# Second layer's input blocks without the row factor 1/rms, which multiplies the products' results

## The chip, the core and the metric

The kernel runs on one core of one Trainium2 chip. The core has a matrix engine (TensorE, PE in the profile; PEld are its weight loads), a vector engine (VectorE, DVE), a scalar engine (ScalarE, ACT), GpSimd (POOL) and SyncE (SP), which here issues nearly all DMAs. The engines run their own instruction streams and wait for one another on semaphores. The metric is the device time of one execution in microseconds, median of the runs.

## The reference

A decoder trunk of two layers on x (1024 tokens by 1024 channels, f32). Each layer normalizes the rows, projects, mixes, gates and projects back:

```python
for i in range(DEPTH):
    hn = rms_norm(h, ln_g[i])            # h * rsqrt(mean(h*h, -1) + EPS) * g
    proj = jnp.einsum('bsd,de->bse', hn, w_in)
    u, q_mem, gate = ...
    y = diff_attention(u, ...) if i == 0 else multiscale_pool(u, ...)
    m = memory_attention(q_mem, mem_n, w_kv[i])
    z = jnp.concatenate([y, m], axis=-1) * jax.nn.silu(gate)
    h = h + jnp.einsum('bse,ed->bsd', z, w_out[i])
return rms_norm(h, final_g)
```

Layer 1 is differential attention with 12 heads of 128. Layer 2 pools u over windows of 2, 4, 8 and 16 tokens in four groups of 384 channels and mixes each group with a 384 by 384 matrix. Both have a memory attention of four heads over 256 memory tokens.

What matters here: the factor 1/rms belongs to a token (a row of h), the gain g to a channel. In a projection, sum over d of h[s,d] * r[s] * g[d] * w[d,e], the factor r[s] can be taken out of the sum and multiply the result.

## The kernel before, in words

All activations lie with channels on the 128 partitions and tokens in the free dimension: h is 8 tiles (d = 0 to 7) by two halves of 512 tokens. Half 1 is computed first. Each f32 operand is split in a high part (rounded by an ACT copy) and a low part (a DVE or POOL difference), and a product of f32 accuracy is three matmuls (`mm3`, L126 to L128): high by high, high by low, low by high.

**The order of the work.** `plan` fills a list of jobs. Each has a load (DMA of weights, splits) and a run that yields steps on PE; the load of job i + 1 is called ahead of the run of job i. PE's order is the program's; the other engines' instructions are put in order by a scheduler that goes by priority (program order, with `high_priority(offset=SOON)` to draw some forward) and its own estimate of times, and so are the DMA issues on SP.

**Layer 1's output projection** is `out_jobs(0)` (L1551). For half 1 and then half 0 it goes through three rounds of d (0 to 2, 3 to 5, 6 and 7), each over all 16 tiles of z (`chunk`, L1588). When a d is complete, `finish` (L1623) loads the matching part of x into a tile `res` (L1629, two slots in layer 1), adds it to the bank (L1640), squares the sum and adds it to a running sum of squares (`accumulate_square`, L503), and stores h to DRAM (L1648). `means` (L1654) turns the sum of squares into row means on PE (L251) and takes the inverse root in a chain of small DVE operations (L225 to L242); `spread` (L1657) broadcasts the factor over the partitions with PE (`row_spread`, L524). For half 1 both run within half 0's first round. `blocks_first` (L1273) then scales half 1's eight tiles by gain and factor (L1265) and splits them, between the chunks of half 0's second round.

**Layer 2's input projection** uses Winograd's form of Strassen's algorithm with 7 products for 8. Rows are the two halves of tokens, columns two weight tiles (a pair), and the sum over d is cut at d = 4. The seven products take the blocks 11, 21 (half 1, d below and from 4), t1 = x12 - x11, t2 = x22 - t1, t3 = x22 - x12, t4 = x21 - t2 and 22 of the hidden state, four tiles each. `product` (L1140) makes one: 12 matmuls from a box of split weights (`split_box`, L1126; six boxes, prepared four products ahead; weights come by DMA into three raw buffers, L1130). Results are joined on the way out of the banks: `keep` (L1188) holds p1, u2 and u3, and `evac0` and `evac1` give the four finished halves of the pair to `mem_query_keep`, `gate_keep` or `pooled_keep`. `land` (L1213) is the step that takes a bank out: an ACT copy, or a DVE addition when there is something to add.

**The passage between the two** is `plan_mixing` (L1038). Four pairs of a memory query and a memory gate (`firsts`) and a pair of u tiles (`lead`) run their products 1 and 2 first, as these need only half 1's blocks. `means0(0)` stands behind the first product and `spread0(0)` behind the third. `spread0(0)` calls `blocks_second` (L1280), with an order of DVE's work written out by hand: scale the eight tiles of half 0 (L1294), form t1, t2, t3, t4 (L1297), split them and 22 (L1257 and L1258). Then come products 6, 7, 5, 4, 3 of the four pairs and the lead, and four groups, each with its pairs of u and gate tiles and its mixing products (`group`, L1466).

**The memory units** (`mem_units`, L696) of layer 2 run between these products, at steps counted from the mark "out0" and written out as a list (L1538): scores with a softmax, transposes, values. Their operands come by DMA into the pool "mem1", whose memory is that of the pool "out0" before it.

**The pooling** (`pooled_keep`, L1420) adds u shifted by 1, 2, 4 and 8 (L1446, the first on POOL), subtracts u (L1451) and splits (L1460, L1461).

## Time and profile before

| | |
|---|---|
| median of 3 runs | 1838.45 us (1836.51 to 1844.82) |
| the profiled execution's own time | 1839.47 us |
| its span | 1837.7 us |
| mean granted PE clock | 0.986 |
| DMA | 188.68 MB, mean 103 GB/s |
| output projection of layer 1 ends | about 1207.9 us |
| groups of layer 2 end, output projection of layer 2 begins | about 1636 us |

The span is what the profiler saw of one execution; its time is 1.8 us longer. Busy time is the time in which an engine has an instruction under way; matmuls are pipelined and their ends are modelled, so they overlap a little. A row of a table of stretches gives the stretch, its length, the busy time (and number of instructions) of PE, PEld, DVE, ACT and POOL, the granted PE clock (1.00 is full), the share of the DMA engines and GB/s. A row of waits gives the waiting engine, tile and line, what ended the wait, the total, the number and the longest. A timeline row gives start, duration, engine, line, operation, output and inputs, shape and count; in brackets is the idle time of the engine before it. A row of a line's instructions gives the shortest, median and longest duration in ns. `pmq_pga12` is the pair of memory query 0 and gate tile 12, with a letter for the bank's role: x (products 1 and 2), y (6), z (7, 4), v (5, 3).

### The profile page before, as it was taken

The page shows a single profiled execution, that of the slowest core. Times are in us where ns is not written, and L with a number is a line of the kernel's source. Part 1 is how long each engine was busy: PE and PEld are TensorE (multiplying, and loading weights), DVE is VectorE, ACT ScalarE, POOL GpSimd, SP SyncE. Part 2 cuts the span into 40 slices and gives each one's busy share as a digit, 9 for nine tenths or more (in the row PEclk, how much of TensorE's full clock was granted, in tenths as well). Part 3 has the DMA queues.
Part 4 walks back from the last instruction along what each step waited for, and adds up shares of the span by engine and source line. Part 5 has one row for each costly group of instructions (what it writes and reads, how often), then busy time and mean ns, then how long its engine had stood idle before and what let it go on. Part 6 is the DMA issues. An engine that isn't in the chain of part 4 may idle for free. (4 is left out here: it accounts for less than half of the span.)

```text
span 1837.7 us, 24949 instructions
## 1 busy us (share of the span) xinstructions
PE 1747.2 (95%) x8634; PEld 1453.9 (79%) x8634; DVE 1219.4 (66%) x2421; ACT 942.2 (51%) x1770; POOL 640.7 (35%) x555
## 2 busy tenths in 40 slices
PE   7799999999999999999989999997999999989997
PEld 5688888888888888888788787875788777767875
DVE  7766676667667667665447677778876767754423
ACT  6667566657657656743246556554533332234422
POOL 4334334343334334333151143500133433413452
PEclk9899999999999999999999999998999999999998
DMA  5011111111111111112462787852312121146542
GB/s 175 33 35 47 39 54 58 35 49 56 35 58 47 35 58 58 36 52 75 149 209 80 241 283 251 285 170 84 111 61 89 61 83 67 54 153 223 164 160 92
DMA packets 83982, 188.68 MB, mean 103 GB/s; under 512 B 9456, under 2 KB 17360, under 8 KB 83856
## 3 DMA queue, kind: packets, MB, share of 16 engines
q1 hardware_dynamic: 81600, 183.08, 30.1%
q10 hardware_dynamic: 2160, 3.75, 0.5%
q8 instruction: 68, 1.11, 0.3%
q14 instruction: 58, 0.48, 0.1%
q0 software_dynamic: 96, 0.26, 0.1%
HBM read 155.29 MB, written 31.77 MB: 102 GB/s over the span
## 5 line engine op out<-in xcount | busy, mean ns | idle before, releaser
L863 ACT ACTIVATE e<-e,st 128x640 f32<-128x640 f32 (+4 forms) x192 | 148.3, 773 | 93.6 <-DVE st L854 92.5
L119 POOL TENSOR_TENSOR wl_o<-wf_o,wh_o 128x288 fp32r<-128x288 f32 (+1 forms) x80 | 110.1, 1377 | 219.9 <-ACT wh_o L116 185.4
L874 POOL TENSOR_SCALAR e<-e,st,coef 128x640 f32<-128x640 f32 (+4 forms) x96 | 89.3, 930 | 169.3 <-DVE st L873 164.6
L1583 DVE TENSOR_TENSOR zr<-zf,zr 128x512 fp32r<-128x512 f32 x132 | 112.4, 866 | 35.4 <-ACT zr L1582 33.7
L119 DVE TENSOR_TENSOR wl_o<-wf_o,wh_o 128x480 fp32r<-128x480 f32 (+1 forms) x80 | 60.3, 754 | 110.6 <-ACT wh_o L116 107.7
L903 ACT CAST wth<-wt 128x512 fp32r<-128x512 f32 (+2 forms) x168 | 71.9, 428 | 107.7 <-PE wt L900 81.4
L1582 ACT CAST zr<-zf 128x512 fp32r<-128x512 f32 x132 | 81.6, 620 | 82.0 <-DMA zf<-z 58.0
L116 ACT CAST wh_o<-wf_o 128x768 fp32r<-128x768 f32 (+1 forms) x80 | 70.1, 876 | 99.4 <-PE ob L127 42.4
L904 DVE TENSOR_TENSOR wtl<-wt,wth 128x512 fp32r<-128x512 f32 (+2 forms) x168 | 83.1, 495 | 55.9 <-ACT wth L903 55.5
L854 DVE CUSTOM_DVE_ANT_0 e<-s,mask 128x512 f32<-128x512 f32 (+2 forms) x192 | 109.2, 583 | 14.5 <-PE s L849 12.4
L849 PE MATMUL s<-kb,qa 128*128 128x512 f32 (+2 forms) x288 | 99.2, 351 | 7.8 <-DVE kb L801 7.2
L126 PE MATMUL ga<-hh,wh_ga 128*128 128x512 f32 x256 | 104.0, 406 | 0.0
L127 PE MATMUL ga<-hl,wh_ga 128*128 128x512 f32 x256 | 100.9, 394 | 0.0
L128 PE MATMUL ga<-hh,wl_ga 128*128 128x512 f32 x256 | 100.9, 394 | 0.0
L849 PE MATMUL s<-kb,qlo 128*128 128x512 f32 (+2 forms) x288 | 98.8, 350 | 0.0
L878 DVE SCALAR_TENSOR_TENSOR e<-e,st,e 128x640 f32<-128x640 f32 (+4 forms) x96 | 80.5, 838 | 14.9 <-POOL e L874 14.2
L126 PE MATMUL k<-hh,wh_k 128*128 128x512 f32 x192 | 80.9, 421 | 8.7 <-ACT wh_k L116 8.7
L126 PE MATMUL oa<-zr,wh_o 128*128 128x512 f32 x192 | 75.8, 395 | 6.2 <-ACT zr L1582 4.2
L128 PE MATMUL oa<-zr,wl_o 128*128 128x512 f32 x192 | 75.3, 392 | 4.7 <-DVE wl_o L119 2.6
L126 PE MATMUL v<-hh,wh_v 128*128 128x512 f32 x192 | 79.6, 414 | 0.0
L127 PE MATMUL k<-hl,wh_k 128*128 128x512 f32 x192 | 76.3, 397 | 3.3 <-DVE hl L499 3.3
L126 PE MATMUL q<-hh,wh_q 128*128 128x512 f32 x192 | 79.2, 413 | 0.0
(1225 smaller groups left out, 5517.9 us busy)
## 6 DMA issues: line engine op xcount, KB each, us to landing
zf<-z SPq DMA_DIRECT2D x132, 256.0 KB
wf_o<-in_w_out SPq DMA_DIRECT2D x64, 384.0 KB
wf_ga<-in_w_in SPq DMA_DIRECT2D x16, 512.0 KB
wf_o<-in_w_out SPq DMA_DIRECT2D x16, 512.0 KB
wf_q<-in_w_in SPq DMA_DIRECT2D x12, 512.0 KB
wf_v<-in_w_in SPq DMA_DIRECT2D x12, 512.0 KB
z<-rs SPq DMA_DIRECT2D x24, 256.0 KB
z<-z SPq DMA_DIRECT2D x24, 256.0 KB
```

What stands on the lines that cost most here:

```text
L119: eng.tensor_tensor(wl[:, c], wf[:, c], wh[:, c].bitcast(F32), op=ALU.subtract)
L126: nc.tensor.matmul(out, sh, mh, start=first, stop=False, skip_group_check=more)
L127: nc.tensor.matmul(out, sh, ml, start=False, stop=False, skip_group_check=more)
L128: nc.tensor.matmul(out, sl, mh, start=False, stop=last, skip_group_check=more)
L849: nc.tensor.matmul(sc[m][:, w], q[half][part][:, m, qs], k[kh][:, m, w], start=(part == 0), stop=(part == 1),)
L854: nc.vector.tensor_tensor_reduce(out=es[m][:, lo:hi], in0=sc[m][:, : hi - lo], in1=self.mask[:, S - n + lo : S - n + hi], scale=1.0, scala ...
L863: nc.scalar.activation(es[m][:, :n], es[m][:, :n], AF.Exp, bias=least[m], scale=-1.0, accum_out=st[:, 2, m : m + 1],)
L874: nc.gpsimd.tensor_scalar(es[1][:, :n], es[1][:, :n], st[:, 3, 1:2], self.coef[:, 1:2], op0=ALU.mult, op1=ALU.mult,)
L878: nc.vector.scalar_tensor_tensor(es[0][:, :n], es[0][:, :n], st[:, 3, 0:1], es[1][:, :n], op0=ALU.mult, op1=ALU.add)
L904: nc.vector.tensor_tensor(wl[:, lo:hi], t[:, lo:hi], wh[:, lo:hi].bitcast(F32), op=ALU.subtract)
L1582: nc.scalar.copy(z[:, 0, :], zf)
L1583: nc.vector.tensor_tensor(z[:, 1, :], zf, z[:, 0, :].bitcast(F32), op=ALU.subtract)
```

## The change

1. **Blocks without 1/rms.** In layer 1's `finish`, the residual sum is made in place in the tile `res`, which now has three slots and is stored from there. ACT writes a copy scaled by the second layer's gain, and `blocks(half, d)` at once makes what can be made of it: the splits of 11 and 21 for half 1; t1 for half 0 with d below 4; t2 and t3 with d from 4.
2. **Late blocks last.** `blocks_last` makes t4 and 22. It stands behind products 1 and 2 of the first two pairs.
3. **The factor on the results.** `spread` copies the factor of each half into a kept tile `rs1`. `land` multiplies with it on DVE: from the bank where there is nothing to add, in place behind the addition otherwise. `keep` (p1, u2, u3) stays without it. The gates' tanh and product now read the tile and not the bank.
4. **Leads over two sets of banks.** Products 1 and 2 of two pairs take turns, one on the banks `pj`, one on `sb`. The lead pair of u tiles no longer runs ahead but in the order of the other pairs.
5. **Means behind the leads.** `means0(0)` stands behind all eight leading products, `spread0(0)` behind product 7 of the first pair, and the mark "out0" there too. The memory units' steps from that mark are 8 lower, one of them 10. Against the first pair's product 6 the first unit then stands 8 steps later.
6. The pooling's edge tile has one slot instead of two, and the squares' tile one instead of two in layer 1.

```diff
-        lead = self.pair(u1(0), u1(1))
-        lead["home"] = lambda: (self.epool, "p1", 1)
-        for p in firsts + [lead]:
+        for p in firsts:
             p["early"] = (1, 2)
-        for i, p in enumerate(firsts):
-            self.product(p, 1)
+        for i in (0, 2):
+            for n in (1, 2):
+                for p, bank in zip(firsts[i : i + 2], (self.pj, self.sb)):
+                    self.product(p, n, bank)
             if i == 0:
-                self.between(lambda: means0(0))
-            if i == 1:
-                self.between(lambda: spread0(0))
-            self.product(p, 2)
-        self.mark("out0")
-        self.product(lead, 1, self.sb)
-        self.product(lead, 2)
+                self.between(self.blocks_last)
+        self.between(lambda: means0(0))
         for p in firsts:
             for n in (6, 7, 5, 4, 3):
-                self.product(p, n, self.sb if n == 6 and p is firsts[0] else None)
+                self.product(p, n)
+                if n == 7 and p is firsts[0]:
+                    self.between(lambda: spread0(0))
+                    self.mark("out0")
...
-    def land(self, t, bank, more):
-
+    def land(self, t, half, bank, more):
+
+        by = self.rs1[:, half * HALF : (half + 1) * HALF]
         with self.tc.high_priority(offset=SOON):
-            if more is None:
-                self.nc.scalar.copy(t, bank)
-            else:
+            if more is not None:
                 self.nc.vector.tensor_tensor(t, bank, more, op=ALU.add)
+                bank = t
+            self.nc.vector.tensor_tensor(t, bank, by, op=ALU.mult)
...
-            if more is not None:
-                self.land(g, bank, more)
-            x = bank if more is None else g
-            nc.scalar.activation(th, x, AF.Tanh, scale=0.5)
-            nc.vector.scalar_tensor_tensor(g, th, 1.0, x, op0=ALU.add, op1=ALU.mult)
+            self.land(g, half, bank, more)
+            nc.scalar.activation(th, g, AF.Tanh, scale=0.5)
+            nc.vector.scalar_tensor_tensor(g, th, 1.0, g, op0=ALU.add, op1=ALU.mult)
...
+    def blocks(self, half, d):
...
+        i = d % 4
+        if half:
+            self.split_block(("11", "21")[d // 4], i, h[1, d], 2 * d, 2 * d + 1, nc.vector)
+            return
+        x11, x21 = h[1, i], h[1, 4 + i]
+        x12 = h[0, i]
+        if d < 4:
+            nc.vector.tensor_tensor(x11, x12, x11, op=ALU.subtract)
+            self.split_block("t1", i, x11, 48 + 2 * i, 49 + 2 * i, nc.vector)
+            return
+        x22 = h[0, d]
+        nc.vector.tensor_tensor(x11, x22, x11, op=ALU.subtract)
+        self.split_block("t2", i, x11, 16 + 2 * i, 17 + 2 * i, nc.vector)
+        nc.vector.tensor_tensor(x12, x22, x12, op=ALU.subtract)
+        self.split_block("t3", i, x12, 24 + 2 * i, 25 + 2 * i, nc.vector)
+
+    def blocks_last(self):
...
+        for i in range(4):
+            nc.vector.tensor_tensor(h[1, 4 + i], h[1, 4 + i], h[1, i], op=ALU.subtract)
+            self.split_block("t4", i, h[1, 4 + i], 44 + i, 40 + i, nc.vector)
+        for i in range(4):
+            self.split_block("22", i, h[0, 4 + i], 32 + i, 36 + i, nc.vector)
...
-            r = pool.tile([P, HALF], F32, tag="res", bufs=2 + layer, name=f"res{nm}")
+            r = pool.tile([P, HALF], F32, tag="res", bufs=3, name=f"res{nm}")
             if layer == 0:
                 nc.sync.dma_start(r, a["x"][half, :, d, :])
...
+                h = r
...
             if layer == 0:
                 nc.sync.dma_start(self.h_dram[d][:, cols], h)
+                if half == 0 and d >= 4:
+                    f = pool.tile([P, HALF], F32, tag=f"hk{d}", name=f"hf{nm}")
+                else:
+                    f = self.slot(32 + (d if half else 8 + d), f"hf{nm}", F32)
+                nc.scalar.activation(f, h, AF.Copy, scale=self.ln_g[1][:, d : d + 1])
+                self.hid[half, d] = f
+                self.blocks(half, d)
...
+            cols = slice(half * HALF, (half + 1) * HALF)
+            if layer == 0:
+                self.keep_spread(half, self.rs1[:, cols])
                 return
```

`blocks_first`, `blocks_second`, `scale_hidden` and `h_order` go.

More of the change, by code (lines that the diff above doesn't have):

```diff
@@ L1085, in plan_mixing @@
             t = 3 * gi
+            pairs(u1(t), u1(t + 1))
             if gi == 0:
-                for n in (6, 7, 5, 4, 3):
-                    self.product(lead, n)
                 self.mark("mem1")
-            else:
-                pairs(u1(t), u1(t + 1))
             pairs(gate1(t), u1(t + 2))
@@ L1188, in keep @@
         def keep(name, a, b=None):
-            pool, tag, bufs = p["home"]() if name == "p1" and "home" in p else (self.epool, "ev", 6)
-            t = pool.tile([P, HALF], F32, tag=tag, bufs=bufs, name=f"{name}{nm}")
+            t = self.epool.tile([P, HALF], F32, tag="ev", bufs=6, name=f"{name}{nm}")
             with self.tc.high_priority(offset=SOON):
-                self.land(t, a, b)
+                if b is None:
+                    nc.scalar.copy(t, a)
+                else:
+                    nc.vector.tensor_tensor(t, a, b, op=ALU.add)
             p[name] = t
@@ L1223, in evac @@
             f = self.epool.tile([P, HALF], F32, tag="ev", bufs=6, name=f"mqf1{m}{half}")
-            self.land(f, bank, more)
+            self.land(f, half, bank, more)
             self.nc.sync.dma_start(self.mq_dram[1][m][:, half * HALF : (half + 1) * HALF], f)
@@ L1429, in evac @@
             u = box["u"]
-            self.land(u[:, PAD + half * HALF : PAD + (half + 1) * HALF], bank, more)
+            self.land(u[:, PAD + half * HALF : PAD + (half + 1) * HALF], half, bank, more)
             box[half] = True
@@ L1453, in pooled @@
             )
-            e = pool.tile([P, PAD], F32, tag="edge", bufs=2, name=f"edge{t}")
+            e = pool.tile([P, PAD], F32, tag="edge", name=f"edge{t}")
             b = win - 1
@@ L1532, in other_layers @@
             with self.pool("ev") as self.epool:
+                self.rs1 = self.epool.tile([P, S], F32, name="rs1")
                 with self.pool("out0") as self.opool:
@@ L1628, in finish @@
                 ssum[half] = []
-            r = pool.tile([P, HALF], F32, tag="res", bufs=2 + layer, name=f"res{nm}")
+            r = pool.tile([P, HALF], F32, tag="res", bufs=3, name=f"res{nm}")
             if layer == 0:
                 nc.sync.dma_start(r, a["x"][half, :, d, :])
-                if half == 0 and d >= 4:
-                    h = pool.tile([P, HALF], F32, tag=f"hk{d}", name=f"hn{nm}")
-                else:
-                    h = self.slot(32 + (d if half else 8 + d), f"hn{nm}", F32)
-                self.hid[half, d] = h
+                h = r
             else:
@@ L1642, in finish @@
             self.accumulate_square(
-                pool, h, ssum[half], d, nm, (("ssum", 1), ("ssum_", 1), ("sqt", 2)),
+                pool, h, ssum[half], d, nm, (("ssum", 1), ("ssum_", 1), ("sqt", 1 + layer)),
                 alone=layer == 1 and half == 0,
@@ L1657, in spread @@
         def spread(half):
-            if layer == 0 and half:
-                bc = self.opool.tile([P, HALF], F32, tag="bc", name=f"bc{half}")
-                hs["first"] = self.blocks_first(self.keep_spread(half, bc))
+            cols = slice(half * HALF, (half + 1) * HALF)
+            if layer == 0:
+                self.keep_spread(half, self.rs1[:, cols])
                 return
-            if layer == 0:
-                with self.tc.high_priority(offset=SOON):
-                    self.blocks_second(self.row_spread(half))
-                return
-            cols = slice(half * HALF, (half + 1) * HALF)
             if half:
@@ L1684, in out_jobs @@
                         self.between(lambda f=(means, spread)[kk // 4]: f(1))
-                    if layer == 0 and half == 0 and r == 1:
-                        self.between(lambda: next(hs["first"]))
         return means, spread
```

73 lines of the change are left out of this document (4 added, 69 removed).

## The prediction

> **What bounds the kernel now.** I read the page's busy shares first, then a table of busy times by stretch, the PE's waits in the stretches that the change touches, and the timeline around the longest wait.
>
> ```profile
> span 1837.7 us, 24949 instructions
> PE 1747.2 (95%) x8634; PEld 1453.9 (79%) x8634; DVE 1219.4 (66%) x2421; ACT 942.2 (51%) x1770; POOL 640.7 (35%) x555
> ```
>
> PE is busy 95% of the span, so the change can only win from the missing 5% or lose by making more of it. The stretches say where it lies:
>
> ```profile
> core 0: us, PE busy (x) PEld busy (x) DVE busy (x) ACT busy (x) POOL busy (x), PEclk, DMA share, GB/s
> 1130.00:1160.00 30.00, 27.64 (x125) 22.37 (x124) 28.06 (x46) 18.83 (x31) 14.85 (x8) 1.00 0.62 196
> 1160.00:1207.90 47.90, 47.90 (x213) 39.64 (x213) 33.23 (x42) 25.68 (x40) 17.47 (x13) 1.00 0.84 293
> 1207.90:1272.40 64.50, 48.71 (x209) 37.93 (x207) 53.88 (x98) 31.73 (x61) 0.22 (x2) 0.89 0.33 106
> 1220.00:1256.00 36.00, 28.61 (x119) 21.57 (x117) 35.67 (x59) 20.79 (x37) 0.22 (x2) 0.98 0.23 71
> 1256.00:1268.00 12.00, 4.26 (x14) 3.54 (x15) 8.47 (x15) 2.28 (x4) 0.00 (x0) 0.50 0.51 160
> 1280.00:1320.00 40.00, 39.39 (x199) 31.79 (x198) 36.24 (x71) 20.95 (x54) 5.75 (x4) 1.00 0.34 110
> 1272.40:1384.00 111.60, 107.97 (x534) 88.43 (x534) 94.55 (x167) 50.38 (x120) 26.40 (x19) 1.00 0.25 84
> 1384.00:1429.00 45.00, 45.00 (x199) 37.02 (x198) 24.55 (x37) 13.90 (x23) 12.99 (x11) 1.00 0.27 91
> 1384.00:1636.00 252.00, 242.63 (x1053) 196.53 (x1052) 178.44 (x224) 77.45 (x125) 90.29 (x67) 1.00 0.22 74
> 1429.00:1456.00 27.00, 25.18 (x110) 20.14 (x109) 23.82 (x28) 9.09 (x14) 13.82 (x10) 1.00 0.18 54
> 1501.00:1529.00 28.00, 24.46 (x105) 19.29 (x104) 25.29 (x27) 8.35 (x13) 14.35 (x10) 1.00 0.14 45
> 1576.00:1604.00 28.00, 25.75 (x112) 20.58 (x111) 25.84 (x28) 7.94 (x13) 15.98 (x9) 1.00 0.17 52
> ```
>
> Layer 1's output projection ends at 1207.9. The next 64.5 us, ten leading products and the first pair's last five, have 48.71 us of PE work: 15.8 idle. From 1220 to 1256 DVE works 35.67 of 36 us, so PE waits for DVE there. The memory units and first u tiles (1272.4 to 1384) lose 3.6 us, the groups behind them (1384 to 1636) 9.4, mostly in three short stretches where DVE is 88 to 92% busy.
>
> ```profile
> PE ms L126 <- ACT mq L629: 8.5, 1, 8.5
> PE pmq_pga12z L126 <- DVE u3pmq_pga L1219: 4.2, 1, 4.2
> PE pmq_pga15x L126 <- ACT p1pmq_pga L1217: 0.7, 1, 0.7
> PE ms_h L251 <- DVE ssq L516: 0.7, 1, 0.7
> ```
>
> ```profile
> 1256.13 0.33 SPq L1137 DMA_DIRECT2D wf_pmq_pga14b<-in_w_in  x1
> 1256.55 0.38 SPq L636 DMA_DIRECT2D mkv<-mk  x1
> 1263.46 0.58 PE L126 MATMUL ms<-mkvr,mq 128*128 128x256 f32 x1 [8.48 <-ACT mq L629]
> ```
>
> Two waits hold 12.7 of the 15.8 us. The fourth block sum is split late, as DVE is full; and the memory operands' load leaves SP only at 1256.55, right behind a weight load whose buffer DVE had been slow to free, and reaches PE 6.9 us later. Behind these waits the granted clock is 0.50 (1256 to 1268): 4.26 us of PE work there would need half, another 2.1.
>
> **The change, part by part.** *Second-layer block sums from 1208 on.* Let T be 1207.9 to 1384, 176.1 us, DVE 53.88 + 94.55 = 148.4. Its unit prices:
>
> ```profile
> 1219.01 2.72 DVE L1294 SCALAR_TENSOR_TENSOR hn<-hn,gains,bc_h 128x512 f32<-128x512 f32 x4 [1.78 <-PE bc_h L528]
> 1251.20 1.90 DVE L1258 TENSOR_TENSOR xt4l<-hn,xt4h 128x512 fp32r<-128x512 f32 x3
> L1217 ACT COPY u<-u_u4x x1: 587/587/587, 1421.1 to 1421.1; 128x512 f32<-128x512 f32 x1
> ```
>
> Scalings run at 0.68 us each (2.72/4), two-input operations at 0.61 ((1.90 - 0.69)/2, a single one shows 0.69). The eight scalings go: -5.4. Block sums with d below 6 need no 1/rms any more and are made in the projection: four differences and four splits for t1, the same for t2 and t3 with d = 4 and 5; 16 x 0.61 = -9.8. Six pairs land in T with four evacuations each; every one gets a DVE multiplication, 24 x 0.61 = +14.6 (a multiplication like this isn't in the trace; the split has the same shape and two inputs). DVE's sum hardly moves: 147.8.
>
> What moves is when it falls due. Before, nothing from scaling on could start until PE had the row means, about 1219; now only d = 6, 7 is left at 1207.9 (8 operations, 4.9 us), and t4 and 22 (12, 7.3 us) follow behind the first two pairs' leads. A product is 12 matmuls, 12 x 45.00/199 = 2.7 us: t2 is wanted after eight, at +22, t4 after eleven and the means, at +32. By +22 DVE owes 4.9 and 17 operations more (two residual sums, two sums of squares, six lead splits, four multiplications, three for product 6): 15.3 us. By +32 come 7.3 and six more (products 7, 5, 4; u2, u3): 26.3 and the means' small chain. It keeps up.
>
> PE's floor in T is 176.1 - 15.8 - 3.6 - 2.1 = 154.6. DVE at 147.8 would be 96% of that. The best stretch with this mix, 1280 to 1320, has DVE 90.6% busy and PE losing 0.6 us. At that fill T takes 147.8/0.906 = 163.1: **-13.0**. Ends: the floor, -21.5; or the memory wait left over with its clock and half the rest, 154.6 + 8.5 + 2.1 + 4.3 = 169.5, so -6.6; I take -5 as the bad end, a little beyond that.
>
> *Leads over two sets of banks, means behind them.* The three 0.7 us waits for ACT to copy p1 (one row above stands for them) and the one at the means go; they are in the 15.8. The means' chain of small DVE operations now has two products, 5.4 us, before spread needs it; what waits is the first multiplication with the second half's factor, and behind it on DVE the next pair's splits. The factor's copy costs ACT one instruction like the 0.587 above: hidden, as ACT is 49% busy in 1207.9 to 1272.4. Without that cover PE would wait up to 5 us once.
>
> *The memory units* start eight steps later against the first pair. Scores come after thirteen products, 35.4 us, and about 2 for means and spread: near 1246. Their load, 6.9 us ahead, must leave SP by 1239. It stands in SP's queue behind the weight load that needs the second pair's boxes split, which needs box slots freed by products that end about 1234 to 1237. So it is nearly even: 0 to 4 us of wait, inside the 8.5 that 163.1 leaves above the floor.
>
> *Output projection.* Gone is a burst that cost PE something:
>
> ```profile
> 1140.02 5.94 DVE L1265 SCALAR_TENSOR_TENSOR hn<-hn,gains,bc 128x512 f32<-128x512 f32 x8
> 1148.99 0.50 PE L128 MATMUL oa<-zr,wl_o 128*128 128x512 f32 x1 [1.95 <-DVE wl_o L119]
> L1257 ACT CAST x11h<-hn x4: 612/615/620, 1140.8 to 1143.6; 128x512 fp32r<-128x512 f32 x4
> ```
>
> Scaling (eight) and splitting half 1 in one go left PE 2.4 us idle in 1130 to 1160 (30.00 - 27.64). Now they are spread over the ends of the rounds: 8 splits, 8 operations for t1, 8 for t2 and t3, 24 for the old 16. The densest place is half 0's second round end, where d = 3, 4, 5 come at once: ten operations, 6.1 us, in the stretch 1160 to 1207.9, where DVE has 47.90 - 33.23 = 14.7 us to spare. ACT gains sixteen scaled copies, at 0.615 like the cast above 9.8 us over the projection, beside its 54% there (25.68 of 47.90). On SP nothing is added: the 16 loads of x and 16 stores of h stay; only the store now reads the tile that the load filled, so a slot of res is free one store later. With three slots each is asked for again a whole round later, so this is hidden; if not, a round's last sum is late, and behind it only copies and splits. I put -2.4 for the old burst, +2.4 for the new one: **0** (-2.4 to +4).
>
> *The groups, 1384 to 1636.* Ten pairs land, 40 multiplications, 24.4 us more for DVE, which has 252 - 178.4 = 73.6 to spare. Where it is full, it hurts: each short stretch gets about six (3.7 us), so 23.82, 25.29 and 25.84 become 27.5, 29.0, 29.5 in 27, 28 and 28 us: 3.0 over.
>
> ```profile
> PE pga_u5z L126 <- DVE u2pga_u L1219: 1.8, 1, 1.8
> PE pga_u8z L126 <- DVE u2pga_u L1219: 1.8, 1, 1.8
> PE pga_u8v L126 <- DVE gap L1241: 1.6, 1, 1.6
> PE pga_u11v L126 <- DVE gap L1241: 1.1, 1, 1.1
> L1128 DVE TENSOR_TENSOR box<-s2pga_u,box 128x512 fp32r<-128x512 f32 x6 | 5.9, 980 | 3.4 <-ACT box L1127 3.4
> L1219 DVE TENSOR_TENSOR gap<-pga_u5v,u2pga_u 128x512 f32<-128x512 f32 x1 | 0.7, 691 | 1.4 <-PE pga_u5v L128 1.4
> ```
>
> The waits on u2 get one u multiplication more in front, +0.6 in each of three groups, +1.8. The two waits on the gate may go: its bank was free after tanh and a product, now after one multiplication, -2.7. Thirty of the forty read two SBUF tensors, as the box split does, which takes 0.98 on average here; operations with a bank as one input stay at 0.69. Fifteen fall into the full stretches: 15 x 0.29 = 4.4, a third of it on PE's path, +1.5. Sum 3.0 + 1.8 - 2.7 + 1.5 = 3.6, taken as **+3.5** (-2.7 to +12, half of 24.4).
>
> [...]
>
> **Sum.** -13.0 + 0 + 3.5 = -9.5 against the profiled execution, 1839.47 us (span 1837.7): 1830.0. The median of the runs, 1838.45, is 1.0 lower: 1829.0.
>
> **The rivals.** (a) *The memory wait stays.* SP's queue keeps the load behind the weights. T then gains 6.6, not 13.0: -6.6 + 3.5 = -3.1, 1835.4. For it: the weight load ahead of it still needs the second pair's boxes, as before. Against: what held the weight load was DVE's full stretch, which is lightened.
>
> (b) *Slower: the multiplications reach PE.* Each lies between a result and its reader, u to the pooled sums, gate to its product. Where nine tenths of the 24.4 us reach PE, it is +22.0 - 13.0 = +9.0, 1847.5; it turns slower from 13.0/24.4 = 53%. For it: PE waits for DVE in all three full stretches. Against: from 1384 to 1429 PE loses nothing with DVE at 24.55 of 45, so about half of the multiplications have room.
>
> (c) *Better: T near its floor, groups free.* The stall falls to a third of what 163.1 leaves, 2.8: T -18.7, groups 0: -18.7, 1819.8. For it: 1280 to 1320 lost only 0.6 at 90.6%. Against: four such stretches in a row would be needed, with DVE at 147.8 of 157.4.
>
> (d) [...] If each of the thirty meets POOL at its share, 90.29/252 = 36%, and then waits out a long one, as one split did (2.43 us, 1.74 over 0.69), 30 x 0.36 x 1.74 = 18.8 us of DVE are lost; with half on PE's path instead of the 1.5, groups cost 2.1 + 9.4 = 11.5: -1.5, 1837.0.
>
> ```profile
> 1436.27 2.43 DVE L1128 TENSOR_TENSOR box<-s2pga_u,box 128x512 fp32r<-128x512 f32 x1
> ```
>
> [...]
>
> **How the numbers follow.** Forecast 0.48, (a) 0.15, (b) 0.13, (c) 0.17, (d) 0.07. A measurement of this kernel can tell about 0.5%, 9.2 us, from no change, so faster means below 1829.3. The forecast lies on that bound; as its term of -13.0 has more room below (to -21.5) than its other terms above, I count 0.31 of 0.48 as faster; with (c) 0.48. Slower takes (b) and 0.03 of the rest: 0.16. Same: 0.36. All unknown costs at their good ends give -21.5 - 2.4 - 2.7 = -26.6 (1812), at their bad ends -5 + 4 + 12 = +11 (1849); leaving out (b)'s upper part and the last of (c) takes 1814 to 1843.
>
> **What would show it.** Right: from 1208 on no wait for the fourth block sum, a memory wait under 4 us, clock 1.00 throughout, T near 163 us with DVE about 90% busy, no 0.7 us waits on p1; 1130 to 1160 without the wait on wl_o, at most one new wait at half 0's second round end; in the groups PE's idle time 12 to 14 us instead of 9.4, its waits on u2 longer, on the gate's product gone. Wrong: the wait on the memory operands still 8 us with a clock of 0.50 behind it (a); PE idle in the groups over 25 us (b); under 3 us of waits in T (c); multiplications beside POOL at 1.5 us or more (d).

## The result, and the profile after

The changed kernel takes 1852.57 us (median of 4 runs, 1849.81 to 1852.87), the kernel before 1838.45 (1836.51 to 1844.82): a ratio of 1.0067, 95% interval 1.0041 to 1.0094. It is slower by over half a per cent, where the prediction had 1829.0.

The page of the profiled execution after, whose own time is 1852.87 us (granted clock 0.981, before 0.986):

```profile
span 1851.1 us, 24987 instructions
PE 1760.9 (95%) x8634; PEld 1463.2 (79%) x8634; DVE 1265.1 (68%) x2467; ACT 947.9 (51%) x1779; POOL 643.6 (35%) x557
```

The span is 13.4 us longer. To find them I cut both spans at the same instructions: the first matmul of layer 1's output projection, the first product of the first pair, product 1 of the gate pair 2, that of the gate pair 11, the first matmul of layer 2's output projection, the end. The table of stretches of the kernel before:

```profile
1025.50:1207.90 182.40, 177.98 (x786) 145.32 (x785) 134.40 (x179) 99.98 (x158) 72.52 (x50) 1.00 0.79 263
1207.90:1385.30 177.40, 157.97 (x747) 127.40 (x746) 149.73 (x267) 82.11 (x181) 26.62 (x21) 0.96 0.29 93
1385.30:1604.80 219.50, 211.52 (x919) 171.67 (x918) 154.09 (x193) 68.35 (x111) 84.33 (x62) 1.00 0.22 73
1604.80:1634.30 29.50, 28.11 (x122) 22.40 (x121) 21.37 (x27) 9.10 (x15) 5.16 (x4) 1.00 0.19 57
1634.30:1837.70 203.40, 183.07 (x809) 148.74 (x807) 76.15 (x124) 72.29 (x105) 75.93 (x58) 0.97 0.52 170
```

and of the changed kernel:

```profile
1024.80:1216.80 192.00, 182.18 (x785) 147.43 (x784) 146.11 (x192) 113.87 (x183) 73.07 (x52) 0.98 0.75 249
1216.80:1389.90 173.10, 161.04 (x748) 131.29 (x748) 145.31 (x258) 75.59 (x167) 29.02 (x21) 0.96 0.28 92
1389.90:1615.20 225.30, 213.89 (x920) 172.54 (x919) 188.69 (x230) 65.38 (x107) 81.76 (x62) 0.99 0.21 71
1615.20:1642.50 27.30, 27.30 (x122) 22.48 (x121) 24.41 (x32) 10.54 (x16) 7.02 (x5) 1.00 0.20 58
1642.50:1851.10 208.60, 187.30 (x809) 150.73 (x807) 77.09 (x124) 72.03 (x105) 76.00 (x58) 0.95 0.51 167
```

The first number behind the stretch is its length, the next PE's busy time; length less busy time is PE's idle time, and a lower clock shows as a longer busy time (PE did 10 matmuls in a busy 3.41 us at 0.50, 17 at 1.00). Layer 1's output projection grew by 9.6 us (5.4 of it idle, 9.82 against 4.42; of the 4.2 busy, two drops of the clock to half, at 1125 and 1204, make 3.4). T, the second row, shrank by 4.3: PE's idle time fell by 7.4 (19.4 to 12.1), but its busy time rose by 3.1, since four short drops now lie where PE works, while the one long drop before, 1254.4 to 1268.1, lay for the most part under the wait of 8.5 us. The groups grew by 5.8, their last pair shrank by 2.2, layer 2's output projection, where no code was changed, grew by 5.2; what lies ahead is 0.7 shorter. That is the 13.4.

PE's waits in T after:

```profile
PE mt L679 <- DVE me L670: 4.0, 2, 2.3
PE bc_h L528 <- DVE rsyh L242: 2.6, 1, 2.6
PE mo L694 <- DVE mwl L685: 2.0, 1, 2.0
PE pga_u2v L126 <- DVE pool L1405: 2.0, 1, 2.0
PE ms L126 <- ACT mkvr L643: 0.7, 1, 0.7
```

The 8.5 us for the memory operands and the 4.2 for the fourth block sum are gone. In their place stand five waits of about 2 us, all for DVE. In the projection two groups of waits are new and among the longest:

```profile
PE oc L127 <- DVE zr L1532: 3.5, 3, 1.7
PE ms_h L251 <- POOL ssq L516: 1.6, 1, 1.6
```

The first is DVE's split of z at the stage's end, the second the means of half 1. The table of stretches and the timeline at the end:

```profile
1188.50:1208.50 20.00, 15.94 (x60) 11.73 (x59) 20.00 (x29) 14.39 (x25) 10.61 (x4) 0.91 0.64 215
```

```profile
1201.28 8.80 POOL L119 TENSOR_TENSOR wl_o<-wf_o,wh_o 128x384 fp32r<-128x384 f32 x1 [5.53 <-ACT wh_o L116]
1210.11 0.33 SPq L1133 DMA_DIRECT2D wf_pmq_pga13e<-in_w_in  x1
1210.55 0.37 SPq L1530 DMA_DIRECT2D zf<-z  x1
1214.86 0.50 PE L126 MATMUL oc<-zr,wh_o 128*128 128x512 f32 x1 [1.31 <-ACT zr L1531]
```

DVE works 20.00 of 20 us. Beside it GpSimd's share of a weight split (L119) takes 8.80 us. When it ends, at 1210.08, SP issues the load of the next layer's weights, which needs that buffer, and only then the last z, which stands behind it in SP's queue; PE waits for that z. SP's own wait, and the same split in the kernel before:

```profile
SPq L1133 <- POOL wl_o L119: 4.4, 1, 4.4
```

```profile
1199.99 1.65 POOL L119 TENSOR_TENSOR wl_o<-wf_o,wh_o 128x384 fp32r<-128x384 f32 x1 [3.70 <-ACT wh_o L116]
```

### The profile page after: what moved, and what is told of

Its sections match the earlier page's. It is cut to its first block, busy times and chain, and to the rows that moved or that the text cites. A ratio compares the mean times of both kernels' runs of the same rounds, so it can differ in the third digit from the quotient of the medians.

```text
span 1851.1 us, 24987 instructions
## 1 busy us (share of the span) xinstructions
PE 1760.9 (95%) x8634; PEld 1463.2 (79%) x8634; DVE 1265.1 (68%) x2467; ACT 947.9 (51%) x1779; POOL 643.6 (35%) x557
## 5 line engine op out<-in xcount | busy, mean ns | idle before, releaser
L119 POOL TENSOR_TENSOR wl_o<-wf_o,wh_o 128x288 fp32r<-128x288 f32 (+1 forms) x80 | 109.7, 1372 | 238.6 <-ACT wh_o L116 205.9
L1532 DVE TENSOR_TENSOR zr<-zf,zr 128x512 fp32r<-128x512 f32 x132 | 116.3, 895 | 35.5 <-ACT zr L1531 33.2
L119 DVE TENSOR_TENSOR wl_o<-wf_o,wh_o 128x480 fp32r<-128x480 f32 (+1 forms) x80 | 60.8, 760 | 111.9 <-ACT wh_o L116 110.3
L878 DVE SCALAR_TENSOR_TENSOR e<-e,st,e 128x640 f32<-128x640 f32 (+4 forms) x96 | 80.5, 838 | 14.9 <-POOL e L874 14.2
```

The source lines that it names most:

```text
L119: eng.tensor_tensor(wl[:, c], wf[:, c], wh[:, c].bitcast(F32), op=ALU.subtract)
L878: nc.vector.scalar_tensor_tensor(es[0][:, :n], es[0][:, :n], st[:, 3, 0:1], es[1][:, :n], op0=ALU.mult, op1=ALU.add)
L1532: nc.vector.tensor_tensor(z[:, 1, :], zf, z[:, 0, :].bitcast(F32), op=ALU.subtract)
```

## The experiments

Lengths are those of the stages above, from each kernel's table of stretches (groups and last pair together), in us. The ratio is to runs of the kernel before on the same chip.

| kernel | median | ratio, 95% interval | projection 1 | T | groups | projection 2 |
|---|---|---|---|---|---|---|
| before, first profile | 1838.45 | | 182.4 | 177.4 | 249.0 | 203.4 |
| before, once more | 1840.03 | 0.9999 (0.9978 to 1.0020) | 184.1 | 178.0 | 248.9 | 203.5 |
| changed | 1852.57 | 1.0067 (1.0041 to 1.0094) | 192.0 | 173.1 | 252.6 | 208.6 |
| changed, once more | 1848.73 | 1.0058 (1.0037 to 1.0078) | 196.7 | 171.9 | 252.4 | 205.3 |
| no multiplications | 1835.14 | 0.9980 (0.9963 to 0.9997) | 191.5 | 158.2 | 252.4 | 206.5 |
| before + 112 multiplications | 1875.93 | 1.0195 (1.0158 to 1.0233) | 182.0 | 200.5 | 264.7 | 207.7 |
| before + 64 multiplications | 1855.15 | 1.0080 (1.0059 to 1.0101) | 183.7 | 187.2 | 253.5 | 206.7 |
| t4, 22 held | 1851.02 | 1.0066 (1.0040 to 1.0092) | 186.9 | 179.3 | 252.8 | 206.9 |
| squares apart | 1846.71 | 1.0053 (1.0036 to 1.0070) | 195.2 | 168.6 | 252.5 | 206.6 |
| multiplications on POOL | 1857.98 | 1.0098 (1.0074 to 1.0122) | 194.9 | 171.5 | 264.4 | 205.0 |
| held + apart + POOL | 1855.82 | 1.0091 (1.0063 to 1.0119) | 191.3 | 174.7 | 264.4 | 204.2 |
| weight split on DVE | 1843.82 | 1.0022 (1.0006 to 1.0038) | 188.1 | 170.0 | 253.9 | 209.3 |
| scale in softmax, shifted | 1846.85 | 1.0030 (1.0015 to 1.0045) | 195.0 | 167.2 | 253.3 | 205.4 |
| + held + apart, shifted | 1846.61 | 1.0044 (1.0026 to 1.0062) | 191.1 | 169.0 | 253.2 | 206.7 |
| leads on one bank set | 1848.90 | 1.0047 (1.0035 to 1.0058) | 191.4 | 173.1 | 252.4 | 206.5 |
| scale in softmax, not shifted | 1844.27 | 1.0022 (1.0001 to 1.0043) | 195.3 | 166.5 | 252.7 | 207.1 |
| split on DVE + softmax | 1837.16 | 0.9982 (0.9968 to 0.9996) | 187.7 | 167.2 | 252.7 | 208.9 |
| + held + apart | 1839.87 | 0.9997 (0.9984 to 1.0010) | 185.3 | 169.1 | 252.4 | 205.9 |
| split on DVE + softmax + apart | 1835.45 | 0.9978 (0.9967 to 0.9990) | 187.3 | 165.4 | 252.8 | 205.9 |
| the same, means early | 1838.12 | 0.9992 (0.9978 to 1.0007) | 186.2 | 165.4 | 252.6 | 208.4 |

**The changed kernel and the one before, each once more.** No edit.

> The changed kernel as it is, once more, for the spread of its own profile. Theory A (the layer's output projection is late because the block sums now lie in it, and most drops of the granted clock follow waits that come in every execution): 1850 to 1853 us; the stage from the projection's start to the first product takes 190 to 194 us again, and the drops at 1124, 1203, 1248, 1288, 1333 and 1343 are there again at the same waits. Rival C (the drops are chance, the same in kind for both kernels): the number of drops changes by three or more between this profile and the last, they follow other waits, and the timed runs lie over 5 us apart.

> The kernel before, unchanged, for a second profile. If the clock's drops outside the changed stages are a matter of the execution: layer 2's output projection takes 203 to 208 us and the drops number two to six beside the tail's, at other places than the first profile's; the output projection of layer 1 takes 182 to 184, T 176 to 180, groups 219 to 221 all the same. If they belong to the change: 203.4 us and no drop beside T's long one and the tail.

The changed kernel's projection came out at 196.7, above theory A's 190 to 194, as the last z came later still (PE waited 3.79 us for it), and the median of 1848.73 lies below its range. Ahead of the tail the clock dropped to half five times instead of nine, three times at the same waits (the means at 1124, the spread, `mo`). So the stage is long in both executions, as theory A has it, and the number of drops changes, as rival C has it; the runs lie 3.8 us apart, less than C's 5. The kernel before repeated all its stages within 1.7 us, layer 2's projection at 203.5, with one short drop beside T's long one. Every other kernel, most of them near the changed one, has 204.2 to 209.3 there. What makes that last term is left open.

**Without the multiplications, and before with them.** The first kernel leaves the factor 1/rms out of the computation. In `land`:

```diff
-            if more is not None:
+            if more is None:
+                self.nc.scalar.copy(t, bank)
+            else:
                 self.nc.vector.tensor_tensor(t, bank, more, op=ALU.add)
-                bank = t
-            self.nc.vector.tensor_tensor(t, bank, by, op=ALU.mult)
```

> The changed kernel without the 64 multiplications by 1/rms (that part of the computation is left out): a result of two banks is an addition, one of a single bank is a copy on ScalarE, as before the change. Theory A: the output projection is untouched by them and stays at 190 to 194 us; the groups go from 225 back to about 219 us, the memory units' stretch gains up to 5 us, so 1838 to 1846 us, still no faster than before. Rival B (the multiplications are the whole loss, and the rest of the change gains what was forecast): 1829 us or less.

> The kernel before with only the multiplications added: all 64 results are multiplied by a column of ones on VectorE (the values stay the same), single banks too, in place of ScalarE's copies. Theory A: the output projection keeps its 182 us; the groups go from 219.5 to about 225 and the memory units lengthen by 1 to 5 us, so 1843 to 1850 us. Rival B: 1850 us or more, with over 10 us in the groups alone.

The first kernel's 1835.14 us lie between both expectations: theory A had given the multiplications too little in T. The second edit caught more than its text says: the helper also serves p1, u2 and u3, so 112 multiplications were added, 48 of them on intermediate sums. Its 1875.93 us decide nothing between the two theories; it shows the dose; the next kernel has the 64 alone:

> The kernel before with exactly the 64 multiplications that the change adds (by a column of ones); the 48 intermediate sums, which the run before this one multiplied too, go without. Priced by the changed kernel with and without them (T 172 or 173 against 158 us, groups 224 or 225 against 221), theory A' (the multiplications cost some 14 us in the memory units and 3 to 5 in the groups, and the output projection nothing): T 188 to 193 us, groups 222 to 225, output projection 182, 1852 to 1858 us. Rival (they cost little where the old block sums still make the waits): 1846 us or less.

T of the kernel without multiplications, and of the kernel before with 64, in the tables of stretches:

```profile
1212.50:1370.70 158.20, 153.47 (x748) 126.43 (x747) 129.92 (x237) 78.58 (x173) 28.12 (x21) 1.00 0.30 101
```

```profile
1206.60:1393.80 187.20, 164.97 (x747) 131.59 (x746) 163.59 (x292) 80.97 (x176) 27.04 (x21) 0.94 0.27 88
```

Read DVE's column, the third. In the changed kernel it loses 15.4 us with the multiplications and T shortens by 14.9 (13.7 by the second profile); in the kernel before it gains 13.9 and T grows by 9.8. So T pays 0.7 to 1.0 us for each us that DVE is given, and the change without its multiplications gains 19.2 us in T. T of 187.2 lies just below the 188 to 193 expected, the time of 1855.15 within 1852 to 1858. In the medians they cost 13.6 to 17.4 us. In the groups the price is less clear: 4.5 us more in the kernel before, none in the changed one, where the execution without them had two drops of the clock, some 3.4 us, and the changed kernel one. The projection stays at 191.5 without them, as theory A had it.

**t4 and 22 held.** A tiny addition ties them to the last residual sum:

```diff
+        for x in [h[1, 4 + i] for i in range(4)] + [h[0, 4 + i] for i in range(3)]:
+            nc.vector.scalar_tensor_tensor(
+                x[:, :1], h[0, 7][:, :1], 0.0, x[:, :1], op0=ALU.mult, op1=ALU.add
+            )
```

> The changed kernel with the t4 and 22 blocks (12 VectorE operations, 8 ScalarE copies) held until the projection's last result: seven additions of zero times that result to one column each tie them to it. Theory A: the burst at 1185 to 1209 is shorter by the six operations that had been drawn forward, the waits at 1196 to 1215 fall from 5.4 to under 2 us and the drop at 1203 goes; the stage takes 185 to 189 us and the whole 1843 to 1848 us. Rival B: no change, 1849 to 1853 us.

The timeline of GpSimd at the projection's end, with the held blocks:

```profile
1198.73 3.86 POOL L119 TENSOR_TENSOR wl_o<-wf_o,wh_o 128x384 fp32r<-128x384 f32 x1 [5.65 <-ACT wh_o L116]
```

The projection is 5 to 10 us shorter, GpSimd's split takes 3.86 us instead of 8.80, and the wait for the last z is gone. But T is 6 to 7 us longer, as the operations that had been drawn forward lie in T again (DVE 150.7 us there for 145.3), and the median doesn't move. The rival had the time right, theory A the stage: what leaves the projection comes back in T.

**The squares apart.** In `accumulate_square`, in layer 1:

```diff
+        if tag == "sqt" and bufs == 1:
+            pool, tag, bufs = self.epool, "ev", 6
```

> The changed kernel with the squares of this output projection in the six slots that the results use later, so that a square no longer waits for GpSimd's addition of the one before (one slot in the change, two before it). Theory A, part two (the one slot is what makes PE wait 1.6 us for the means at 1124 and what delays ScalarE's copies behind it): that wait and its drop of the clock go, the projection takes 3 to 6 us less, 186 to 190 us, the whole 1844 to 1848. Rival (the backlog is VectorE's alone): projection 190 to 196 us, 1848 to 1853.

PE's wait for the means and its drop go, as expected, but not the stage's length, 195.2 us where 186 to 190 were expected: GpSimd's split takes 9.63 us this time and the wait for the last z is 4.53. The backlog at the end decides. T is 3 to 4 us shorter than in the changed kernel; why stays open.

**The weight split on VectorE.** In `chunk`:

```diff
-                w = self.load_w(..., n, dve=5 * n // 8)
+                dve = n if layer == 0 and half == 0 and r == 2 else 5 * n // 8
+                w = self.load_w(..., n, dve=dve)
```

> The changed kernel with GpSimd's share of the low weight parts of the last four chunks of layer 1's output projection (384 of 1024 columns each) on VectorE. Theory D (beside VectorE's unbroken row of block operations GpSimd's share takes 8.8 to 10.1 us instead of 1.0 to 1.7; SyncE's load of the next layer's weights waits for that buffer, and the last input's load stands behind it on the same queue; that is PE's wait of 1.3 to 4.5 us at 1215): the wait goes, VectorE gets 2 us more of work in its densest place, the projection takes 188 to 192 us, 1843 to 1848 in all. Rival (VectorE's backlog alone makes the waits): projection 193 to 198 us, 1849 to 1853.

The timeline of SP in this kernel, and its stretch:

```profile
1198.22 0.33 SPq L1133 DMA_DIRECT2D wf_pmq_pga13e<-in_w_in  x1
1198.83 0.32 SPq L1530 DMA_DIRECT2D zf<-z  x1
```

```profile
1018.70:1206.80 188.10, 181.20 (x786) 147.54 (x785) 145.39 (x192) 113.04 (x183) 60.49 (x48) 0.98 0.78 254
```

The last z leaves right behind the weights, 180.1 us after the stage's start instead of 185.8, and the wait for it is gone, though DVE got GpSimd's columns (its busy time in the stage is 145.4 us, in the changed kernel 146.1). Theory D holds: the projection is 3.9 and 8.6 us shorter than in the two profiles of the changed kernel. About 5 us above the kernel before remain.

**The queries' scale in the softmax.** `mem_query_keep` no longer multiplies; `rq` holds 1/rms by the softmax scale, one column for 128 tokens:

```diff
-        nc.vector.tensor_scalar(st[:, 0, :], st[:, 0, :], -MSCALE, None, op0=ALU.mult)
+        nc.vector.scalar_tensor_tensor(st[:, 0, :], st[:, 0, :], -1.0, rq, op0=ALU.mult, op1=ALU.mult)
...
-                e[:, i, :], sc[i], AF.Exp, bias=st[:, 0, i : i + 1], scale=MSCALE,
+                e[:, i, :], sc[i], AF.Exp, bias=st[:, 0, i : i + 1], scale=rq[:, i : i + 1],
```

> The changed kernel without the eight multiplications of memory queries: their scores' tokens lie on the partitions, so 1/rms goes into the exponential's scale and its bias, which cost no instruction more than two of 4 columns; a single bank of queries is copied by ScalarE again. Theory A' (T pays VectorE's added work nearly in full: 24 or 25 multiplications cost 14 to 15 us): eight fewer give 4 to 5.5 us in T, 167 to 168 us, nothing elsewhere, 1843 to 1846. Rival (only the multiplications on the way of a PE wait count): T 171 to 173, 1847 to 1851.

> The changed kernel with the queries' scale in the softmax, t4 and 22 held until the projection's end, and the squares apart. Theory A, A' and D together: projection 185 to 190 us, T 170 to 174 (the held blocks lengthen T by 3 to 6, the spared multiplications shorten it by 5), groups 223 to 225, 1836 to 1844: level with the kernel before. Rival (what leaves the projection comes back in T in full, and the rest is spread over executions): 1845 to 1850.

T came out at 167.2: eight multiplications are worth 4.7 to 5.9 us there, as theory A' had it; the median of 1846.85 lies just above its range. The kernel with three edits came out in its rival's range, 1846.61, with 191.1 in the projection where 185 to 190 were expected. And the projection of both had more work for PE: with the scale in the softmax 183 us (186.5 busy at a mean clock of 0.98), in the changed kernel 179 (182.2 at 0.98), for the same code. PE's timeline in the middle of the projection, changed kernel and then this one, first and eighteenth of a row of matmuls:

```profile
1049.83 0.39 PE L127 MATMUL oa<-zr,wh_o 128*128 128x512 f32 x1
...
1053.69 0.39 PE L126 MATMUL oa<-zr,wh_o 128*128 128x512 f32 x1
```

```profile
1049.81 0.39 PE L127 MATMUL oa<-zr,wh_o 128*128 128x512 f32 x1
...
1053.77 0.40 PE L126 MATMUL oa<-zr,wh_o 128*128 128x512 f32 x1
```

Seventeen steps take 3.86 us there (0.227 each) and 3.96 here (0.233). `rq` is a tile of 8 columns, 32 bytes, ahead of the projection's buffers. In the next kernel it lies in a tile that is no longer read (`self.rq = self.ln_g[0]`):

> The changed kernel with the queries' scale in the softmax, the 8 columns in a tile that is no longer read, so that no buffer is shifted by 32 bytes. If the shift slowed the matmuls: they come 0.227 us apart again, PE's work in the projection is 179 us, the whole 1839 to 1845. If it was the edit: 0.233 us and 183 us again, 1845 to 1848.

The matmuls of 60 us, in the tables of stretches of the shifted and the unshifted kernel:

```profile
1044.00:1104.00 60.00, 60.00 (x259) 48.20 (x258) 45.64 (x54) 36.58 (x59) 25.02 (x19) 1.00 0.81 263
```

```profile
1044.00:1104.00 60.00, 60.00 (x266) 49.52 (x265) 46.91 (x56) 38.49 (x62) 25.03 (x19) 1.00 0.85 277
```

PE is busy all the time at full clock in both, with 259 and 266 matmuls. Step by step, the stage's matmuls of 512 columns at full clock come 0.234 us apart (median) in both shifted kernels and 0.227 in the other 18 profiles, two of these on the same chip as the shifted ones. So the shift slowed them by some 2.9%, 4 to 5 us of PE's work in the stage. The stage's length doesn't show it, 195.0 us shifted and 195.3 not, as PE is idle for 8.5 us in the one and 12.7 in the other; how much of the missed expectation above is due to the shift is thus open. Why an address matters here the runs don't show.

**Multiplications on GpSimd**, alone and with the held blocks and the squares apart:

```diff
-                bank = t
-            self.nc.vector.tensor_tensor(t, bank, by, op=ALU.mult)
+                self.nc.gpsimd.tensor_tensor(t, t, by, op=ALU.mult)
+            else:
+                self.nc.vector.tensor_tensor(t, bank, by, op=ALU.mult)
```

> The changed kernel with the 48 multiplications of two-bank results on GpSimd; VectorE keeps the 16 of single banks. Theory A' (the multiplications cost what they add to VectorE's queue in the memory units): VectorE's work in T falls from 145 to about 132 us and T from 172 to 160 to 165, groups 220 to 224, 1836 to 1843 us. [...]

> The changed kernel with three edits together: t4 and 22 held until the projection's end, the squares apart, the two-bank multiplications on GpSimd. If the losses are apart as theory A and A' have them: projection 182 to 186 us, T 160 to 168, groups 220 to 224, 1828 to 1838 us, so level with the kernel before or faster. Rival (the work only moves from one stage to the next): 1842 or more.

Shortest, median and longest duration of 24 of these multiplications, those of the gates, on VectorE in the changed kernel and on GpSimd here:

```profile
L1218 DVE TENSOR_TENSOR gap<-gap,rs x24: 660/689/2401, 1254.5 to 1635.5; 128x512 f32<-128x512 f32 x24
```

```profile
L1217 POOL TENSOR_TENSOR gap<-gap,rs x24: 1287/1667/2276, 1258.1 to 1647.7; 128x512 f32<-128x512 f32 x24
```

DVE's busy time in T falls by 1.8 us only (143.5 in 238 instructions against 145.3 in 258, where about 132 were expected), so its other operations took longer there, beside GpSimd's 54.0 us of work for 29.0; why, no run shows. T came out at 171.5 and the median at 1857.98, where 160 to 165 and 1836 to 1843 were expected, and the groups grow by 12. The three edits together take 1855.82 us, with 191.3 in the projection and 174.7 in T, where 1828 to 1838 were expected: there the rival holds.

**The leads on one set of banks**, the old order:

```diff
-        for i in (0, 2):
-            for n in (1, 2):
-                for p, bank in zip(firsts[i : i + 2], (self.pj, self.sb)):
-                    self.product(p, n, bank)
+        for i, p in enumerate(firsts):
+            for n in (1, 2):
+                self.product(p, n)
...
```

> The changed kernel with the order of the first four pairs as before the change: each pair's two first products back to back, all in one set of two banks, the late blocks behind the second pair. Theory A: PE waits about 0.7 us for each pair's kept sum as before the change, four times, so T 174 to 177 us and 1851 to 1855 in all. Rival (the pairing buys nothing in this kernel): T 171 to 173, 1848 to 1852.

PE waits for p1 again, four times (1.05 us once, 0.68 three times), but T is 173.1 as with the pairing: the rival. In exchange the wait for the spread, 2.6 us, is gone. DVE's work, not these banks, sets T.

**Both causes mended, and what else adds to it.** The weight split and the softmax together; then with t4 and 22 held and the squares apart; with the squares apart alone; and that with `means0` behind the first two pairs' leads:

> The changed kernel with both mended causes: the low weight parts of the last four chunks on VectorE, and the queries' scale in the softmax, its 8 columns kept in a tile that is no longer read. If the causes are apart: projection 187 to 190 us, T 164 to 168, groups 224 to 226, 1835 to 1841 us, level with the kernel before. Rival (what one saves the other takes back): 1843 or more.

> The kernel with both causes mended, and t4 and 22 held until the projection's end and the squares apart. If the rest of the projection's loss is these blocks and the one slot: projection 183 to 187 us, T 166 to 170, 1832 to 1840 us. Rival (they only move into T): the same as the kernel without these two edits, within 3 us.

> The kernel with the low weight parts on VectorE and the scale in the softmax, and the squares apart, nothing held. If the one slot costs what the wait for the means at 1119 shows (2.0 us and the drop of the clock behind it, 1.7): projection 183 to 186 us, T 166 to 168 as without the squares, 1831 to 1837 us, faster than before the change. Rival (the slots of later results that the squares use are missed elsewhere, or ScalarE's backlog makes the same wait with another name): 187 us or more and 1836 to 1840.

> The kernel of the first run with half 0's means between the first two pairs' leads and the last two, so that the chain to 1/rms starts some 10 us earlier, in VectorE's densest place. If the place behind the leads is what spares PE a wait: PE waits 1 to 3 us for the means or the late blocks' operands come later, 1834 to 1840. If it costs instead (the spread then comes too late for PE): the wait for the spread goes, T 164 to 166, 1829 to 1835.

The two causes are apart: 187.7 and 167.2 us are about what each gave alone (188.1 and 166.5). The held blocks and the squares save 2.4 more in the projection, of which T takes 1.9 back, and the median is 2.7 longer: the rival. With the squares alone the kernel takes 1835.45 us, 0.22% faster than the one before, the lowest median of the kernels that leave nothing out, though its interval overlaps with that of the kernel without the squares (its first two stretches):

```profile
1018.50:1205.80 187.30, 180.05 (x786) 144.77 (x785) 145.73 (x193) 112.92 (x183) 60.35 (x48) 1.00 0.77 254
1205.80:1371.20 165.40, 157.10 (x747) 127.66 (x746) 140.96 (x251) 80.36 (x172) 28.59 (x21) 0.99 0.29 98
```

Its expectation of 183 to 186 us in the projection failed: the wait for the means went with its drop, the length stayed. The place of the means makes no difference in T (165.4 both), and the median of 1838.12 is no shorter.

## Why the prediction was wrong, point by point

- **T, -13.0: measured -4.3, and the step that failed is the fill, with the clock in it.** DVE's sum was nearly right: 147.8 predicted, 145.3 measured. It was divided by 0.906, the share of the best stretch of 40 us. Measured, DVE's busy time over T is 0.844 before (149.73/177.4) and 0.839 after (145.31/173.1), and 0.82 to 0.89 in every kernel here, from 129.9 to 178.9 us of work. With 0.844 the prediction's own sum gives 147.8/0.844 = 175.1, which is -1 against its 176.1. The fill only sums up what PE loses. In PE's terms, 163.1 left 8.5 us above the floor for waits and nothing for the clock; measured are 12.1 us of idle time and four drops. The part of the mechanism on the old block sums was right: their waits are gone, and without the multiplications T is 19.2 us shorter than before. But the multiplications take 13.7 to 14.9 of that back. I had booked both in DVE's sum and then let the stall go as if the sum had fallen.
- **The clock, "1.00 throughout": wrong.** 0.96 in T as before, only in four short drops instead of a long one. The prediction put this term at nothing; the four make up to 6.8 us.
- **Output projection, 0: measured +9.6.** "Ten operations, 6.1 us" with 14.7 to spare, t4 and 22 "behind the first two pairs' leads": the scheduler drew four of the late blocks forward, as their inputs were there, and DVE was full for 20 us. The 14.7 us were the slack of a stretch of 48 us, not of the 20 that counted. What reached PE came in part by DVE's late split of z (3.5 us) and the means (1.6), and in part by a way that the step didn't name: GpSimd's 8.80 us, SP's queue, the last z (1.3 us in this execution, 3.8 in the next). "On SP nothing is added" was true and beside the point. The weight split on DVE and the held blocks each remove that chain. Some 5 us remain, with waits on `zr` and `wl_o` in the dense place; their cause stays open.
- **Groups, +3.5: measured +3.6** (249.0 to 252.6), PE's idle time 11.4 for 9.4 where 12 to 14 was forecast. The waits on u2 became shorter, not longer (1.8 to 0.5 and 0.3), those on the gate's product didn't go but became waits on its multiplication (1.6 and 1.2), new ones on u3 and on the bank's additions came, and nearly half of the term, 1.6 us, is a drop of the clock. So the size was met by other parts than those reckoned, by luck.
- **The last projection, +5.2, had no term.** Its waits are the same but for 0.9 us more on `wh_o` at its start; two drops of the clock that the kernel before doesn't have there make 3.4 us. The cause stays open.
- **The rivals.** (a) fell: `mkv` left SP at 1246.72 and PE waited 0.7 us. (Of the eight steps of the memory units two are 8 lower and six are 10 lower, not one; the first unit does start eight steps later.) (b) had the direction right and the place wrong: the multiplications reach PE in T, not in the groups. (c) fell: the five waits in T make 10.6 us. (d) came for DVE, and small for PE. Of the 64 multiplications 18 take 1.06 to 2.40 us, 11 of them over 1.5; each began while GpSimd had an operation under way and ended 0.55 us behind that operation's end. The other 46 take 0.66 to 0.69 us. In the groups 14 of 40 are long, 13.3 us in all above 0.69 each, where (d) reckoned 18.8; but the groups grew by 3.6 us, not by its 11.5. GpSimd's and DVE's rows at the longest one, and beside the split of 2.43 us in the kernel before:

```profile
1535.83 2.23 POOL L1394 TENSOR_TENSOR ws<-u 128x1039 f32<-128x1039 f32 x1 [1.11 <-DVE u L1218]
1536.21 2.40 DVE L1218 TENSOR_TENSOR gap<-gap,rs 128x512 f32<-128x512 f32 x1
```

```profile
1436.23 1.92 POOL L1446 TENSOR_TENSOR ws<-u 128x1039 f32<-128x1039 f32 x1 [1.24 <-DVE edge L1456]
1436.27 2.43 DVE L1128 TENSOR_TENSOR box<-s2pga_u,box 128x512 fp32r<-128x512 f32 x1
```

In the projection, where (d) had no term, the long operation was GpSimd's: its split takes 8.80 to 10.09 us beside DVE's unbroken row, 3.86 beside a shorter one and 1.65 in the kernel before. What makes these operations long no run here shows.

## What to carry to other kernels

Where one engine's work sets a stage's time, reckon that time from its fill over the whole stage (here 0.82 to 0.89), not over its best stretch, and give the clock a term where waits of about 2 us remain (here 39 of 79 waits of 1.9 to 2.2 us had a drop behind them). Work that is moved in counts like work that is moved out (here T paid 0.7 to 1.0 us for each us on VectorE). Work that "is ready early" can be drawn forward by a scheduler into a stage that looks idle; ask which slow engine beside it releases a buffer that a DMA queue is waiting for, with other loads behind (here GpSimd's split of 8.80 us held SP's queue for 4.4 us, and the last z with it). A factor that belongs to a partition of a later result can go into an activation's scale there (here, in place of eight multiplications on VectorE, T took 166.5 us for 173.1 and 171.9).

## What the runs showed of the hardware

**In the 20 profiles the granted clock was 0.50 behind 70 of 70 windows of 3.41 us with over 1.95 us of idle time on PE.** The same wait of 2.10 us, same instruction, left the clock alone before the change and halved it after. The timeline row, the window or two in which the wait lies, and the window behind it, before and after:

```profile
1764.31 0.50 PE L128 MATMUL oa<-zr,wl_o 128*128 128x512 f32 x1 [2.10 <-POOL wl_o L119]
...
1759.58:1762.99 3.41, 2.62 (x12) 1.85 (x10) 0.69 (x1) 0.78 (x1) 3.41 (x3) 1.00 0.41 154
1762.99:1766.41 3.42, 2.10 (x9) 1.75 (x10) 1.56 (x3) 0.84 (x2) 2.03 (x3) 1.00 0.71 223
1766.41:1769.82 3.41, 3.41 (x17) 2.81 (x16) 1.17 (x2) 3.41 (x6) 2.37 (x2) 1.00 0.99 326
```

```profile
1775.79 0.50 PE L128 MATMUL oa<-zr,wl_o 128*128 128x512 f32 x1 [2.10 <-POOL wl_o L119]
...
1773.90:1777.32 3.42, 1.53 (x7) 1.27 (x8) 0.99 (x2) 0.27 (x1) 2.60 (x3) 1.00 0.57 178
1777.32:1780.73 3.41, 3.41 (x10) 2.64 (x9) 1.63 (x3) 3.41 (x7) 1.79 (x2) 0.50 1.05 317
```

Before, the wait is spread over two windows, which leave PE idle for 0.8 and 1.3 us; after, 1.9 us fall into one, and the next runs at half clock, which costs 1.7 us (half of 3.41). The windows are read off the granted clock: in the 20 traces each of the 382 stretches of one clock, the first and last of an execution left out, is a whole number of 3.41 us long. This wait of 2.10 us comes in all 20 profiles. In ten a drop followed, and there 1.89 to 2.10 us of it lay in one window; in ten none did, and there it was 1.16 to 1.94. Counted over all windows at full clock between 1015 and 1815 us, by PE's idle time in them:

| PE idle in the window, us | number | half clock in the next |
|---|---|---|
| under 1.55 | 4242 | 5 |
| 1.55 to 1.95 | 96 | 39 |
| over 1.95 | 70 | 70 |

For single waits, wherever they lie, this makes a matter of chance of it. With a drop counted where the 3 us behind a wait have a mean clock under 0.9, in the same profiles:

| PE's wait, us | number | with a drop |
|---|---|---|
| 0.6 to 1.3 | 217 | 14 |
| 1.3 to 1.6 | 86 | 6 |
| 1.6 to 1.9 | 63 | 17 |
| 1.9 to 2.2 | 79 | 39 |
| 2.2 to 3 | 39 | 23 |
| over 3 | 21 | 21 |

By these counts a wait of about 2 us costs, on the mean, an estimated 0.8 us more than it lasts (39 of 79 times 1.7), which no term of the prediction held.

**32 bytes ahead of the buffers** made the matmuls of a stage 2.9% slower at full clock (0.234 us apart for 0.227), with no wait that the profile shows.
